# Delta rule: the 16x16 diagonal blocks of I + M inverted by DVE, by way of DRAM, in place of three doubling levels on PE

## The chip, the cores and the metric

The kernel runs on one core of a Trainium2 chip. The metric is the device time of one execution in microseconds (us). The engines are PE (matrix products), DVE (elementwise work on 128 partitions), ACT (activation functions, copies, casts), POOL, and SP, which here only issues transfers; 16 DMA engines move the data between DRAM and the on-chip memory.

## The reference, cut to what matters

Two transformer blocks run one after the other on 256 rows of width 1024. The first is a hybrid layer: attention beside a gated delta rule. The second has a mixer of two kinds of attention and then a mixture of 32 experts. Only the delta rule of the first block is touched. Its core, for each of 8 heads and each chunk of rows, is a triangular system:

```python
def gated_deltanet(q, k, v, g, beta):
    ...
    m = jnp.where(strict, jnp.einsum('bhnid,bhnjd->bhnij', k_beta, kc) * decay, 0.0)
    a_mat = m + jnp.eye(c, dtype=m.dtype)
    rhs = jnp.concatenate([vc * bc[..., None], k_beta * jnp.exp(G)[..., None]], axis=-1)
    sol = lax.linalg.triangular_solve(a_mat, rhs, left_side=True, lower=True, unit_diagonal=True)
    u, w = sol[..., :dv], sol[..., dv:]
    ...
```

The result u, w then feeds a recurrence over the chunks. The inputs q, k, v come from one projection of the normalised input, a causal convolution of width 4, and silu.

## The kernel before

**The first block** takes about the first 400 us. Its big matrix `w_in` is read in pieces of 1 MB (512 rows by 512 columns of float32). A piece is loaded by `load()` (L110, on SP's queue, three buffers), and `piece()` splits it in two parts: ACT casts it to the rounded half `whi` (L309), DVE subtracts to get the rest `wlo` (L310). PE then multiplies with three products for each pair of operands, hi x hi, hi x lo, lo x hi: `proj_T_g` (L204 to L206, 48 products with 256 columns for a piece, output transposed) and `proj_tok_g` (L168 to L170, with 512 columns, output by rows). Near the start stands a small load of the same matrix, 16 columns for beta and the decay: 128 x 8 runs of 64 bytes, 64 KB. The convolution's evacuation on DVE (L533, L535, L540) follows every pair of pieces of the q, k, v of the delta rule.

**The delta rule** is written as a generator, `gdn_half`, for half of the heads (4) at a time. The kernel's chunk is 128 rows, so there are two, t = 0 and 1. For each, the decayed product M is formed transposed, as MT (L604 the product, L605 the decay mask). T, the inverse of I + M, is then built by doubling: blocks of size s on the diagonal are already inverted, and one level joins two neighbours into a block of 2s. The levels are 2, 4, 8, 16, 32, 64; the start is the inverse of the 2x2 blocks, which is I - M with one entry of each block kept (L611, L612 with the table `nm1t`, transposed at L298, copied at L616). One level, for both t and 4 heads, is: 8 + 8 products of MT with the even blocks (L626), a mask on DVE (L628, twice), 8 + 8 products with the transposed T (L641), a subtraction into T on DVE (L642, twice), and, for the next level, 8 transposes of T (L298) with two copies on ACT (L647). The last level, s = 64, ends with L635 and L636 instead. The names in the trace: `Ts` holds T, `TT` its transpose, both among the tiles called `w`.

**The order.** A helper, `together`, runs `gdn_half` and the attention beside the projections: it advances each such generator by one step, then lets the projection go on until 2.5 units of its work are issued. On each engine the order of instructions is fixed when the program is built. Between two groups of a level on PE stand 24 products of a projection. SP issues every load in one order and stands at a load until its buffer is free. The projections of the second half of the heads, the gates and the attention are what runs beside the delta rule; behind them stand the branch products, the mixer, and from about 590 us the experts, which stream 1 MB pieces of weights without a break.

Of the kernel before, what the change touches and what calls it, by code (L numbers as in the profile page):

```python
# [7 lines left out]
F32 = mybir.dt.float32  # L8
# [4 lines left out]
ALU = mybir.AluOpType  # L13
AX = mybir.AxisListType

P = 128
# [1 line left out]
D = 1024  # L18
NEG = -1e30
EPS = 1e-6  # L20
LEVELS = (2, 4, 8, 16, 32, 64)


def _consts():

    import numpy as np

    r = np.arange(P)[:, None]
    c = np.arange(P)[None, :]
    cols = {}  # L30

    cols["ident"] = r == c
    cols["nhalf"] = np.full((P, 16), -0.5)
    cols["iota"] = np.broadcast_to(c[:, :64], (P, 64))
    cols["fold"] = (r % 64) == np.arange(64)[None, :]
    cols["ones"] = np.ones((P, P))
    cols["ustr"] = r < c
    cols["uinc"] = r <= c
    cols["lstr"] = r > c
    cols["cneg"] = np.concatenate([np.zeros((P, P)), np.where(c <= r, 0.0, NEG)], 1)  # L40
    cols["nm1t"] = -((c % 2 == 1) & (r == c - 1)).astype(np.float32)
    lv = []
    for s in LEVELS:
        even = np.array([j for j in range(P) if (j // s) % 2 == 0])[None, :]
        lv.append((r // s == even // s + 1))
    cols["levels"] = np.concatenate(lv, 1)
    half = 16
    inv = np.power(np.float32(500000.0), -np.arange(half, dtype=np.float32) * np.float32(2.0 / 32))
    ang = np.arange(S, dtype=np.float32)[:, None] * inv[None, :].astype(np.float32)
    co, si = np.cos(ang).astype(np.float32), np.sin(ang).astype(np.float32)  # L50
    cols["cosa"] = np.concatenate([co[:P], co[:P], co[P:], co[P:]], 1)
    cols["sina"] = np.concatenate([-si[:P], si[:P], -si[P:], si[P:]], 1)
    inv2 = np.float32(10000.0) ** (-np.arange(0, 32, 2, dtype=np.float32) / np.float32(32))
    cols["inv2"] = np.broadcast_to(inv2[None, :], (P, 16))
    off, at = {}, 0
    for k, v in cols.items():
        off[k] = (at, v.shape[1])
        at += v.shape[1]
    arr = np.ascontiguousarray(np.concatenate([np.asarray(v, np.float32) for v in cols.values()], 1))
    return arr, off  # L60


_CARR, _COFF = _consts()


@with_exitstack
def tile_net(ctx: ExitStack, tc: tile.TileContext, a: dict, dbg=None):
    nc = tc.nc
    V, A, G, T, SY = nc.vector, nc.scalar, nc.gpsimd, nc.tensor, nc.sync
# [13 lines left out]
    def cc(k):  # L83
        o, n = _COFF[k]
        i = max(i for i in range(3) if cuts[i] <= o)
        return ctab[i][:, o - cuts[i]:o - cuts[i] + n]

    ident = cc("ident")
# [207 lines left out]
    def transpose(out, in_):  # L296
        k = in_.shape[0]
        T.transpose(out, in_, ident[:k, :k])  # L298

    def bc(ap, n):  # L300

        return ap[:, :, None].broadcast_to([ap.shape[0], ap.shape[1], n])

    def bm(ap, n):

        return ap[:, None, :].broadcast_to([ap.shape[0], n, ap.shape[1]])
# [92 lines left out]
    with ExitStack() as c1:  # L399
# [4 lines left out]
        w = Pool(wk, **NB)  # L404
# [3 lines left out]
        ps = pm.tile([P, P], F32, name="pm")  # L408
# [21 lines left out]
        ps = pm.tile([P, P], F32, name="pm")  # L430
# [116 lines left out]

        oTb = [None, None]

        def four(f):  # L550
            ps = pm.tile([P, 4, P], F32, name="pm")
            for j in range(4):
                f(j, ps[:, j])
            return ps
# [4 lines left out]
        def gdn_half(hh, cq, ck, cv):  # L559
# [5 lines left out]
            MT, QK, TT, Ts = [], [], [], []  # L565
            for t in range(2):
# [5 lines left out]
                ps = heads4(lambda j: gl[:, j], lambda j: uinc)  # L572
# [4 lines left out]
                for nm, src, sc in (("q", cq, P ** -0.5), ("k", ck, None)):  # L577
                    dst = tk[nm] = w.tile([P, 4, P], F32, name="w2")
                    ps = four(lambda j, o: transpose(o, src[:, j, ts]))
# [4 lines left out]
                    r = rsqrt(ss, 4, 1.0, 4 * EPS, "l_r")  # L584
# [8 lines left out]
                ps = four(lambda j, o: transpose(o, cv[:, j, ts]))  # L593
                V.tensor_tensor(vb[:, t], ps, bc(hbet[:, t, hs], P), ALU.mult)
                yield 0.0
                for src, dst in ((tk["k"], KT[:, :, ts]), (kb, KQ[t][:, :, 0]), (tk["q"], KQ[t][:, :, 1])):
                    ps = four(lambda j, o: transpose(o, src[:, j]))
# [3 lines left out]
                for b in range(2):  # L601
                    ps = pm.tile([P, 2, 2, P], F32, name="pm")
# [3 lines left out]
                                    dm[:, 2 * b:2 * b + 2, None, :].broadcast_to([P, 2, 2, P]), ALU.mult)  # L606
                MT.append(mq[:, :, 0])
                QK.append(mq[:, :, 1])

                tt = w.tile([P, 4, P], F32, name="w2")  # L610
                V.tensor_tensor(tt, MT[t], bm(cc("nm1t"), 4), ALU.mult)  # L611
                V.tensor_tensor(tt, tt, bm(ident, 4), ALU.add)  # L612
                yield 0.0
                ps = four(lambda j, o: transpose(o, tt[:, j]))
                tn = w.tile([P, 4, P], F32, name="w2")
                A.copy(tn, ps)  # L616
                TT.append(tt)
                Ts.append(tn)
                yield 0.0
            for li, s in enumerate(LEVELS):  # L620
                ev = [Ts[t].rearrange("p h (b o s) -> p h b o s", o=2, s=s)[:, :, :, 0] for t in range(2)]
                ys, pss = [], []
                for t in range(2):
                    ps = pm.tile([P, 4, 64], F32, name="pm")
# [6 lines left out]
                if s == 64:  # L631
                    for t in range(2):
                        ps = pm.tile([P, 4, 64], F32, name="pm")
# [4 lines left out]
                for t in range(2):  # L638
                    ps = pm.tile([P, 4, 64], F32, name="pm")
# [4 lines left out]
                for t in range(2):  # L644
                    ps = four(lambda j, o: transpose(o, Ts[t][:, j]))
                    tt = w.tile([P, 4, P], F32, name="w2")
# [6 lines left out]
            ps = heads4(lambda j: TT[0][:, j], lambda j: vb[:, 0, j])  # L653
            A.copy(vn[0], ps)
            yield 0.0
            ps = heads4(lambda j: kdec[:, j], lambda j: vn[0][:, j])
# [1066 lines left out]
```

## Time and profile before

| | us |
|---|---|
| median of 3 runs | 1589.14 (1588.45 to 1589.35) |
| the profiled execution | 1589.79 |
| its span in the trace | 1588.0 |
| PE busy in the span | 1456.5 (92%) |
| DVE busy | 621.5 (39%) |
| ACT busy | 421.8 (27%) |

The span is the time from the first to the last recorded instruction; the execution has 1.79 us around it. PE's share of 92% is an average over stages with different limits, so the windows below count more than the table. DVE and ACT have much idle time in total, spread over the span in short gaps between operations.

### The profile page before, as it was taken

The page shows a single profiled execution, that of the slowest core. Times are in us where ns is not written, and L with a number is a line of the kernel's source. Part 1 is how long each engine was busy: PE and PEld are TensorE (multiplying, and loading weights), DVE is VectorE, ACT ScalarE, POOL GpSimd, SP SyncE. Part 2 cuts the span into 40 slices and gives each one's busy share as a digit, 9 for nine tenths or more (in the row PEclk, how much of TensorE's full clock was granted, in tenths as well). Part 3 has the DMA queues.
Part 4 walks back from the last instruction along what each step waited for, and adds up shares of the span by engine and source line. Part 5 has one row for each costly group of instructions (what it writes and reads, how often), then busy time and mean ns, then how long its engine had stood idle before and what let it go on. Part 6 is the DMA issues. An engine that isn't in the chain of part 4 may idle for free. (4 is left out here: it accounts for less than half of the span.)

```text
span 1588.0 us, 20479 instructions
## 1 busy us (share of the span) xinstructions
PE 1456.5 (92%) x8162; PEld 902.3 (57%) x8162; DVE 621.5 (39%) x1183; ACT 421.8 (27%) x648; POOL 26.0 (2%) x39
## 2 busy tenths in 40 slices
PE   6999999999979989999889989899998889898877
PEld 5889899999779875433424433443443344232325
DVE  6867766456746653302212202221322121220226
ACT  4553554344546631101101101110111010010014
POOL 0000010000000000000000000000000000000000
PEclk9999999999989989999999999999999999999998
DMA  6433233345525179999999999999999999999982
GB/s 211 160 133 124 90 107 107 108 139 193 175 83 186 54 275 388 421 420 421 420 421 419 420 420 421 421 421 420 420 420 421 420 420 420 421 420 421 421 339 93
DMA packets 99247, 484.89 MB, mean 305 GB/s; under 512 B 10470, under 2 KB 14060, under 8 KB 49996
## 3 DMA queue, kind: packets, MB, share of 16 engines
q1 hardware_dynamic: 99004, 483.14, 76.6%
q8 instruction: 66, 1.08, 0.3%
q0 software_dynamic: 144, 0.39, 0.1%
q14 instruction: 33, 0.27, 0.0%
HBM read 482.46 MB, written 1.05 MB: 304 GB/s over the span
## 5 line engine op out<-in xcount | busy, mean ns | idle before, releaser
L1316 PE MATMUL ph<-raw,xs 128*64 128x512 f32 x928 | 233.7, 596 | 6.7 <-DMA raw<-in_w_gu_dram 6.6
L1316 PE MATMUL ph<-whi,xs 128*64 128x512 f32 (+1 forms) x568 | 192.8, 594 | 1.4 <-DMA whi<-in_w_gu_dram 1.3
L1316 PE MATMUL ph<-wlo,xs 128*64 128x512 f32 (+1 forms) x552 | 187.3, 594 | 3.4 <-DMA wlo<-in_w_gu_dram 3.3
L310 DVE TENSOR_TENSOR wlo<-raw,whi 128x2048 fp32r<-128x2048 f32 (+4 forms) x73 | 158.0, 2166 | 79.8 <-ACT whi L309 79.6
L204 PE MATMUL pm<-w,whi 128*128 128x256 f32 x640 | 183.3, 287 | 2.9 <-ACT w L309 2.0
L205 PE MATMUL pm<-w,whi 128*128 128x256 f32 x640 | 180.3, 282 | 2.2 <-DVE w L310 2.2
L206 PE MATMUL pm<-w,wlo 128*128 128x256 f32 x640 | 179.9, 282 | 2.6 <-DVE wlo L310 2.6
L1503 DVE COPY hs<-ph 128x512 f32<-128x512 f32 x34 | 23.5, 692 | 405.0 <-PE ph L1316 405.0
L309 ACT CAST whi<-raw 128x2048 fp32r<-128x2048 f32 (+4 forms) x73 | 132.0, 1808 | 156.2 <-PE pm L205 90.0
L1316 PE MATMUL pm<-raw,act 128*64 128x512 f32 x528 | 150.4, 611 | 23.7 <-DMA raw<-in_w_dn_dram 23.0
L1316 PEld LDWEIGHTS ph<-raw,xs 128*64 128x64 f32 x928 | 74.7, 138 | 141.9 <-issue 127.2
L1503 ACT COPY hs<-ph 128x512 f32<-128x512 f32 x34 | 19.9, 585 | 413.3 <-PE ph L1316 413.3
L1406 DVE SCALAR_TENSOR_TENSOR yl<-pm,gs,yh 128x512 fp32r<-128x512 f32 x34 | 25.4, 749 | 265.1 <-ACT yh L1405 264.4
L204 PEld LDWEIGHTS pm<-w,whi 128*128 128x128 f32 x640 | 122.3, 191 | 3.7 <-ACT w L309 2.4
L206 PEld LDWEIGHTS pm<-w,wlo 128*128 128x128 f32 x640 | 122.6, 192 | 3.1 <-DVE wlo L310 3.0
L205 PEld LDWEIGHTS pm<-w,whi 128*128 128x128 f32 x640 | 122.5, 191 | 2.9 <-DVE w L310 2.8
L1316 PEld LDWEIGHTS ph<-whi,xs 128*64 128x64 f32 (+1 forms) x568 | 62.0, 140 | 83.6 <-issue 76.9
L1316 PE MATMUL pm<-whi,act 128*64 128x512 f32 (+1 forms) x248 | 95.3, 611 | 13.6 <-DMA whi<-in_w_dn_dram 13.6
L1316 PEld LDWEIGHTS ph<-wlo,xs 128*64 128x64 f32 (+1 forms) x552 | 59.3, 140 | 85.0 <-issue 77.4
L1316 PE MATMUL pm<-wlo,act 128*64 128x512 f32 (+1 forms) x248 | 95.0, 597 | 11.4 <-DMA wlo<-in_w_dn_dram 11.4
L1316 PEld LDWEIGHTS pm<-raw,act 128*64 128x64 f32 x528 | 44.9, 139 | 103.7 <-issue 60.6
L1405 ACT ACTIVATE yh<-pm,gs 128x512 fp32r<-128x512 f32 x34 | 23.2, 686 | 282.1 <-PE pm L1316 280.6
(395 smaller groups left out, 1988.7 us busy)
## 6 DMA issues: line engine op xcount, KB each, us to landing
raw<-in_w_gu_dram SPq DMA_DIRECT2D x116, 1024.0 KB, 19.8
whi<-in_w_gu_dram SPq DMA_DIRECT2D x71, 1024.0 KB, 19.8
wlo<-in_w_gu_dram SPq DMA_DIRECT2D x69, 1024.0 KB, 19.9
raw<-in_w_dn_dram SPq DMA_DIRECT2D x66, 1024.0 KB, 19.8
raw<-in_w_in_dram SPq DMA_DIRECT2D x46, 1024.0 KB, 5.1
wlo<-in_w_dn_dram SPq DMA_DIRECT2D x31, 1024.0 KB, 19.8
whi<-in_w_dn_dram SPq DMA_DIRECT2D x31, 1024.0 KB, 19.7
raw<-in_w_branch_a_dram SPq DMA_DIRECT2D x4, 1024.0 KB
```

Of the source, the lines that this page charges most:

```text
L204: T.matmul(o, hi[:, k, ns], xh[:, k0 + k], start=first, stop=False)
L205: T.matmul(o, hi[:, k, ns], xl[:, k0 + k], start=False, stop=False)
L206: T.matmul(o, lo[:, k, ns], xh[:, k0 + k], start=False, stop=last)
L309: A.copy(hi, src)
L310: (by or V).tensor_tensor(lo, src, hi.bitcast(F32), ALU.subtract)
L1316: return tc.keep_in_program_order(T.matmul(*x_, **y_))
L1405: A.activation(yh[:, ns], yp[n_], AF.Copy, scale=b["gs"])
L1406: V.scalar_tensor_tensor(yl[:, ns], yp[n_], b["gs"], yh[:, ns].bitcast(F32), ALU.mult, ALU.subtract)
L1503: (V.tensor_copy if j // 2 else A.copy)(b["hs"][j // 2][:, j % 2 * 512:j % 2 * 512 + 512], hp[j])
```

## The change

The levels are cut to 16, 32 and 64. In place of the three lower ones the 64 blocks of 16x16 on the diagonals (2 chunks x 4 heads x 8 blocks) are inverted by DVE, one block on one partition, by forward elimination: a copy of identities, then for each of 15 columns one multiplication and one subtraction. Since a block's rows lie on 16 partitions, they are moved through DRAM: MT is written out (256 KB for each t), the blocks are read as 64 partitions of 16 rows of 64 bytes, and the inverses are written into a DRAM tile of zeros, from which two full tiles of T are read back. From them TT comes by transposes, as before.

```diff
-LEVELS = (2, 4, 8, 16, 32, 64)
+LEVELS = (16, 32, 64)
+B = 16
...
-    cols["nm1t"] = -((c % 2 == 1) & (r == c - 1)).astype(np.float32)
...
+    cols["eyes"] = np.broadcast_to(np.eye(B).reshape(1, B * B), (P, B * B))
...
+        BS = B * P + B
+        dr = c1.enter_context(tc.tile_pool(name="dr", bufs=1, space=bass.MemoryType.DRAM))
+        whole = dr.tile([8, P // B * BS], F32, name="whole")
+        diag = dr.tile([8, P // B * BS], F32, name="diag")
+        def plain(d, t):
+            return d[t * 4:t * 4 + 4, :P * P].rearrange("h (r c) -> r h c", c=P)
+        def blocks_of(d):
+            v = d.rearrange("g (b r) -> (g b) r", r=BS)[:, :BS - B]
+            return v.rearrange("g (i c) -> g i c", c=P)[:, :, :B]
+        zero = w.tile([P, 4, P], F32, name="w2")
+        V.memset(zero, 0.0)
+        for t in range(2):
+            SY.dma_start(plain(diag, t), zero)
+        def inverse(X, out):
+            V.tensor_copy(out, cc("eyes")[:64].rearrange("p (r c) -> p r c", r=B))
+            tmp = w.tile([P, B, B], F32, name="w1")[:64]
+            for j in range(B - 1):
+                n, m = B - 1 - j, j + 1
+                o = out[:, m:, :m]
+                V.tensor_tensor(tmp[:, :n, :m], bc(X[:, j, m:], m), bm(out[:, j, :m], n), ALU.mult)
+                V.tensor_tensor(o, o, tmp[:, :n, :m], ALU.subtract)
...
                                     dm[:, 2 * b:2 * b + 2, None, :].broadcast_to([P, 2, 2, P]), ALU.mult)
                 MT.append(mq[:, :, 0])
                 QK.append(mq[:, :, 1])
-
+                SY.dma_start(plain(whole, t), MT[t])
+                yield 0.0
+            X = w.tile([P, B, B], F32, name="w1")[:64]
+            SY.dma_start(X, blocks_of(whole))
+            yield 0.0
+            Y = w.tile([P, B, B], F32, name="w1")[:64]
+            inverse(X, Y)
+            yield 0.0
+            SY.dma_start(blocks_of(diag), Y)
+            yield 0.0
+            for t in range(2):
+                tn = w.tile([P, 4, P], F32, name="w2")
+                SY.dma_start(tn, plain(diag, t))
+                Ts.append(tn)
+            yield 0.0
+            for t in range(2):
+                ps = four(lambda j, o: transpose(o, Ts[t][:, j]))
                 tt = w.tile([P, 4, P], F32, name="w2")
-                V.tensor_tensor(tt, MT[t], bm(cc("nm1t"), 4), ALU.mult)
-                V.tensor_tensor(tt, tt, bm(ident, 4), ALU.add)
-                yield 0.0
-                ps = four(lambda j, o: transpose(o, tt[:, j]))
-                tn = w.tile([P, 4, P], F32, name="w2")
-                A.copy(tn, ps)
+                A.copy(tt, ps)
                 TT.append(tt)
-                Ts.append(tn)
-                yield 0.0
+            yield 0.0
             for li, s in enumerate(LEVELS):
                 ev = [Ts[t].rearrange("p h (b o s) -> p h b o s", o=2, s=s)[:, :, :, 0] for t in range(2)]
                 ys, pss = [], []
```

The table of constants that is loaded at the start shrinks by 64 columns. In the lines of after, which are the same code some lines later, PE's products are L205 to L207 (projection) and L669, L684 (the level), the transposes L299, DVE's split L311 and MT's product with its mask L635, L636.

On PE, in the first half, a level's groups and the fills between them. Before, `w_843` and `w_1051` are MT of the two chunks, `w_872` and `w_1103` are T:

```order
L206 MATMUL pm<-w_88,wlo 128x256
L626 MATMUL pm<-w_872,w_843 128x64 x4
L626 MATMUL pm<-w_1103,w_1051 128x64 x4
L204 MATMUL pm<-w_89,whi 128x256
...
L206 MATMUL pm<-w_89,wlo 128x256
L641 MATMUL pm<-w_1134,w_852 128x64 x4
L641 MATMUL pm<-w_1141,w_1060 128x64 x4
```

After, at the place where the first transposes of the blocks' inverses stand (`w_1185` and `w_1187` are the two tiles read back), 12 products L169 to L171 and 196 of L205 to L207 behind the second chunk's L635:

```order
L635 MATMUL pm<-w_678,w_679 128x256 x4
L169 MATMUL pm<-whi,w_89 128x512
...
L205 MATMUL pm<-w_88,whi 128x256
L299 MATMUL pm<-C_66,w_1185 128x128 x4
L206 MATMUL pm<-w_90,whi 128x256
L207 MATMUL pm<-w_88,wlo 128x256
L205 MATMUL pm<-w_88,whi 128x256
L299 MATMUL pm<-C_66,w_1187 128x128 x4
L669 MATMUL pm<-w_1185,w_851 128x64 x4
L669 MATMUL pm<-w_1187,w_1038 128x64 x4
```

The 24 products that stood between two groups of a level have moved together into one long run ahead of the transposes; behind it some groups have 3 between them, others 23 to 26. In the second half 192 projection products stand there, together with transposes and 8 products of the attention.

On DVE, the same place. Before, between MT's mask and the second level (`xpad` belongs to the convolution):

```order
L605 TENSOR_TENSOR w_1051<-pm,w_892 128x512 x2
L310 TENSOR_TENSOR wlo<-raw,whi 128x2048
L611 TENSOR_TENSOR w_1060<-w_1051,C_144 128x512
L612 TENSOR_TENSOR w_1060<-w_1060,C_66 128x512
L628 TENSOR_TENSOR w_1134<-pm,C_144 128x256
L628 TENSOR_TENSOR w_1141<-pm,C_144 128x256
L310 TENSOR_TENSOR wlo<-raw,whi 128x2048
L642 TENSOR_TENSOR w_872<-w_872,pm 128x128x2
```

After, `w_1060` are the blocks and `w_1097` their inverses:

```order
L636 TENSOR_TENSOR w_1038<-pm,w_873 128x512 x2
L573 COPY w_1097<-C_144 64x256
L311 TENSOR_TENSOR wlo<-raw,whi 128x2048
L578 TENSOR_TENSOR w_1099<-w_1060,w_1097 64x15
L579 TENSOR_TENSOR w_1097<-w_1097,w_1099 64x15
...
L578 TENSOR_TENSOR w_1099<-w_1060,w_1097 64x8x8
L311 TENSOR_TENSOR wlo<-raw,whi 128x2048
L579 TENSOR_TENSOR w_1097<-w_1097,w_1099 64x8x8
L534 TENSOR_SCALAR w_1064<-xpad,vT 128x256
...
L579 TENSOR_TENSOR w_1097<-w_1097,w_1099 64x15
L311 TENSOR_TENSOR wlo<-raw,whi 128x2048
```

One split stands ahead of the 30 operations, one in the middle of them, and the next behind the last; from the middle on the convolution's operations alternate with them. In the second half the operations of the attention's softmax stand among them instead, with two splits ahead of the inverse and one in it.

On SP's queue, where before 38 loads of `w_in` stand in a row, after:

```order
L640 DMA whole<-w_851 128x4x128
L111 DMA raw<-in_w_in_dram 128x4x512 x3
L640 DMA whole<-w_1038 128x4x128
L645 DMA w_1060<-whole 64x16x16
L111 DMA raw<-in_w_in_dram 128x4x512 x2
L650 DMA diag<-w_1097 64x16x16
L111 DMA raw<-in_w_in_dram 128x4x512
L654 DMA w_1185<-diag 128x4x128
L654 DMA w_1187<-diag 128x4x128
L111 DMA raw<-in_w_in_dram 128x4x512 x6
```

The new transfers have come in among the loads, and each waits at its place for what it moves: L645 for both writes of `whole`, L650 for the inverse, L654 for L650.

## Rows read from the trace of the kernel before

**Rows 1.** The windows: busy us per engine, PE clock, DMA share, GB/s, of two stretches
```profile
100.00:400.00 300.00, 297.45 (x2404) 286.37 (x2403) 188.14 (x269) 139.51 (x189) 9.06 (x9) 1.00 0.39 127
590.00:1520.00 930.00, 852.80 (x3996) 358.64 (x3995) 209.15 (x504) 102.50 (x165) 1.92 (x3) 0.99 1.01 419
```

**Rows 2.** The waits from 100 to 400 us: engine, line, releaser, total us, times, longest
```profile
PE pm L298 <- DVE w L684: 1.7, 2, 1.5
PE pm L205 <- DVE w L310: 0.3, 1, 0.3
...
DVE wlo L310 <- ACT whi L309: 47.8, 19, 5.2
```

**Rows 3.** PE's timeline through one level: start us, duration, operation
```profile
116.05 1.89 PE L626 MATMUL pm<-w,w 128*128 128x64 f32 x16
117.95 0.28 PE L205 MATMUL pm<-w,whi 128*128 128x256 f32 x1
...
120.66 1.90 PE L641 MATMUL pm<-w,w 128*128 128x64 f32 x16
...
122.56 0.28 PE L205 MATMUL pm<-w,whi 128*128 128x256 f32 x1
...
125.27 1.03 PE L298 MATMUL pm<-C,w 128*128 128x128 f32 x8
...
126.26 0.28 PE L205 MATMUL pm<-w,whi 128*128 128x256 f32 x1
```

**Rows 4.** The groups by line up to 560 us: busy us, mean ns of one
```profile
L626 PE MATMUL pm<-w,w 128*128 128x64 f32 x192 | 22.7, 271 | 0.0
...
L641 PE MATMUL pm<-w,w 128*128 128x64 f32 x160 | 18.9, 271 | 0.0
...
L628 DVE TENSOR_TENSOR w<-pm,C 128x256 f32<-128x256 f32 x24 | 10.1, 423 | 17.2 <-PE pm L626 17.2
```

**Rows 5.** DVE's timeline, near 22, 110 and 130 us
```profile
22.92 0.18 DVE L456 TENSOR_SCALAR angk<-ang 128x32 f32<-128x32 f32 x1
23.13 0.18 DVE L457 TENSOR_SCALAR angk<-angk 128x32 f32<-128x32 f32 x1
...
109.95 0.69 DVE L605 TENSOR_TENSOR w<-pm,w 128x512 f32<-128x512 f32 x1 [0.17 <-PE pm L604]
110.56 2.29 DVE L310 TENSOR_TENSOR wlo<-raw,whi 128x2048 fp32r<-128x2048 f32 x1
...
130.10 0.61 DVE L533 TENSOR_SCALAR w<-xpad,vT 128x256 f32<-128x256 f32 x2
130.63 2.46 DVE L535 SCALAR_TENSOR_TENSOR w<-xpad,vT,w 128x256 f32<-128x256 f32 x6
```

**Rows 6.** Transfers: SP's issue, the windows, the list of DMA issues
```profile
16.38 0.43 SPq L110 DMA_DIRECT2D raw<-in_w_in_dram  x1
...
18.00:19.00 1.00, 0.99 (x4) 1.00 (x5) 1.00 (x2) 0.21 (x1) 0.00 (x0) 0.50 0.73 57
...
raw<-in_w_in_dram SPq DMA_DIRECT2D x46, 1024.0 KB, 5.1
...
out_dram<-hs SPq DMA_DIRECT2D x4, 256.0 KB, 2.2
```

**Rows 7.** The windows around three stretches in which PE stood
```profile
16.10:18.00 1.90, 0.00 (x0) 0.00 (x0) 1.90 (x3) 1.76 (x1) 0.00 (x0) 0.89 0.19 17
19.00:20.50 1.50, 1.50 (x9) 1.50 (x8) 1.50 (x1) 0.00 (x0) 0.00 (x0) 0.50 0.85 276
...
436.00:439.00 3.00, 0.00 (x0) 0.00 (x0) 1.06 (x3) 1.92 (x5) 0.55 (x1) 1.00 0.00 0
441.00:447.00 6.00, 5.38 (x17) 4.87 (x18) 2.98 (x7) 1.44 (x3) 0.55 (x1) 0.50 0.00 0
450.00:452.00 2.00, 0.24 (x3) 0.08 (x1) 2.00 (x2) 0.80 (x3) 0.00 (x0) 1.00 0.00 0
```

## The prediction, made blind

> **What bounds the kernel now.** I read three views in this order: the busy time by stretch, the waits of the engine that is busiest there, and the timeline of that engine around the changed code. By stretch there are two regimes. From 100 to 400 us, where both halves of the delta rule lie, PE is busy 297.45 of 300 us and the DMA engines carry only 0.39 of what they could; from 590 us to the end of the experts the DMA engines are full (1.01) [rows 1]. So the changed code sits in a stretch that PE sets, and whatever PE is spared there moves everything behind it forward, the expert stream included, since its buffers come free that much earlier. The waits say the same: PE waits 1.7 us for the delta rule's output and 0.3 us for a split piece in 300 us, while DVE waits 47.8 us for ACT's casts [rows 2], that is, DVE has slack, but slack handed out in small portions.
>
> **What is removed.** Three of six levels, in two halves. One level on PE is two groups of 16 products and one of 8 transposes, and between the groups stand 24 projection matmuls, which I call fills. From the second fill after one group to the next group are 23 fill steps: 120.66 - 117.95 = 2.71 us, 0.118 each; 24 cost 2.83. From the start of L626's group to the second fill behind it are 1.90 us, less one step 1.79; for L641's group the same 1.79; for the transposes 0.99 - 0.12 = 0.87 [rows 3]. A level is 4.45 us of PE, three are 13.35, and both halves 26.7. The counts confirm that six levels are there: L626 192 = 6 x 2 x 16 products, L641 five times as many as 32 [rows 4]. Since PE waits for nothing there, this is time of the span. On DVE the masks and subtractions of these levels, 0.42 us each [rows 4], and the two old passes over MT (L611, L612) go; DVE isn't the bound there, so I count that at nothing.
>
> **What is added, and whether it is covered.** The new chain of one half is: MT to DRAM, the 16x16 blocks back to 64 partitions, 31 dependent DVE operations, the blocks to DRAM, two tiles back, transposes. It hides behind the fills that the program puts between the last MT matmuls and those transposes. I count from t0, the end of these matmuls.
>
> First half, PE: 12 fills of 512 columns (as two of 256, 0.236 each: 2.8 us) and 196 of 256 columns (23.1 us): PE arrives at the transposes at t0 + 26. The pieces of 48 fills (5.7 us) begin at 2.8, 8.5, 14.1 and 19.8, and each needs its split on DVE first.
>
> First half, DVE and DMA, from rows: two MT operations of 0.69 [rows 5], to 1.4. A 256 KB write to DRAM lands in 2.2 us [rows 6] (the output's), with 0.4 of issue: 4.0. For the reading of 1024 runs of 64 bytes the nearest row is a load with as many runs of 64 bytes, issued at 16.38, with its traffic in 18 to 19 us (share 0.73, 57 GB/s) [rows 6], so about 2.5 us: 6.4 to 6.9. Meanwhile the second piece is split (2.29 a piece [rows 5]), which stands ahead of the inverse on DVE and waits for its cast; I put its end at 7.8. Then 30 small operations. Dependent ones on 128x32 start 0.21 apart (22.92 to 23.13) [rows 5]; the upper bound is an operation on 128x256 at 0.42 [rows 4]. The inverse's views have 14 to 64 elements a partition, so I take 0.21: 6.3 us. In between stand another split (2.2) and 4 + 10 operations of the convolution (0.61 for two, 2.46 for six [rows 5]: 5.3). Sum: 21.6. Only then comes the split of the piece that PE wants at 19.8; in part the small operations fit between the others' dependences, so I take its end at 23.0 and **a PE stall of 3.2 us** (2 to 4). The blocks' write goes out at about 21.5; no row shows 64-byte runs written to DRAM, and I take the load's 2.5 us, the lower bound being the 2.2 of the plain write and the upper open (rival C). Then a 1 MB load, which SP has queued ahead, and the two 256 KB reads: 1 MB takes 5.1 us to land [rows 6], so the reads land about 29 us, just when the stalled PE arrives: **0.5 us** (0 to 2).
>
> Second half: 192 fills and 2.7 us of transposes stand in between: PE arrives at t0 + 25.4. A third split stands ahead of the inverse, which starts at about 10.8, shares DVE with five softmax operations and a split, and ends near 21.4; the write lands at 24, the reads behind their 1 MB load at 27 to 30. **Stall 3.0 us** (1.5 to 4.5).
>
> Three small items. In the remaining levels only 3 fills (0.35 us) instead of 24 now stand at some joints, while a pair of DVE operations takes 0.75: **1.5 us** in both halves (0 to 3). The zeroing of one 128x512 tile on DVE and its two writes stand in the start-up, where PE waits for DVE's first split: **0.5** (0.1 to 0.7, the longer end being any 128x512 operation). And the clock: after PE had been idle from 16.1 to 18.0 us its granted clock was 0.50, the 1.2 GHz level, in 18 to 20.5; after 436 to 439 idle it was 0.50 in 441 to 447; after 450 to 452, with 0.24 busy, it stayed at 2.4 GHz [rows 7]. Two stalls of 3 us lie between these; I let one fall and lose half of 3 us: **1.5** (0 to 6). The additional traffic, some 1.5 MB in 300 us, finds the DMA engines at 0.39 and costs nothing; behind them, SP, which issues all loads in order, stands for some 14 us at the blocks' write for the inverse, with three pieces already loaded (17 us of PE work), so nothing runs dry unless the inverse is late by more than that.
>
> What the Trainium skill says against the 64-byte writes: "DMA: Bandwidth & Descriptors", Specifications, puts the smallest transfer at line rate at 512 bytes and says that below it the engine reads, modifies and writes. No run here shows such a write. If each of them cost the 64-byte load's transfer of about 1 us once more, the estimate by this page would be 2 us on the sum.
>
> **Sum.** 26.7 - (3.2 + 0.5 + 3.0 + 1.5 + 0.5 + 1.5 = 10.2) = 16.5 us. Against the profiled execution, 1589.79 us, that gives 1573.3; it lies 0.65 above the median of the runs shown, so against that 1572.6, and I say **1572.5 us**.
>
> **The rivals.**
> A, all is hidden: splits and reads come in time, as PE's tiny waits of now suggest [rows 2]. Then the whole 26.7 is gained: 1562.4. Against it stands the in-order DVE, which has a split behind the inverse in both halves. Chance 0.13.
> B, DVE becomes the bound: the small operations cost 0.42 instead of 0.21, or the inverse starts later since its blocks come late. 30 x 0.21 = 6.3 us per half more, each of them a stall, since the split behind the inverse is already late: 1572.5 + 12.6 = 1585.1; half of it 1579. Chance 0.14 for 1577 to 1585.
> C, slower: the four transfers with 64-byte runs. Each us that one takes beyond 2.5 is a us on the chain, in both halves, and PE has no more fills to give. From 16.5 / 4 = 4.1 us more each, 6.6 a transfer, the change loses; at 9 us each it is 1572.5 + 26 = 1598.5. For it: 1024 runs with a price not seen in writing. Against it: the load of the same runs had its traffic within about a us. Chance 0.08.
> D, it is no gain since something else sets the end of the stretch, or B and C meet in the middle: 1589. Against it: PE at 297 of 300 us. Chance 0.03.
>
> **How the numbers follow.** My forecast (1566 to 1577) has 0.62. A comparison of this kernel can tell about 0.2%, 3.2 us, from no change. Faster: 0.62 + 0.13 + 0.14 = 0.89; the same: D, 0.03; slower: C, 0.08. The range goes from rival A's end, 1562.5, to the middle of B, 1582, and leaves out the upper part of B, C and D: some 0.17.
>
> **What would show it.** Right: L626's successor runs 96 times instead of 192, PE's waits in 100 to 400 us name a split (L311) late behind the inverse once in each half, some 3 us each, and the transposes wait for the reads by about as much in the second half; the expert stream starts some 16 us sooner and is as long as before. Wrong: the inverse's operations well above 0.21; the writes of blocks landing after 4 us or more; a PE wait of more than 5 us in either half; the clock at its lower level for more than 3 us in the stretch; or a longer start-up than 0.5 us.

## The result, and the profile after

The changed kernel takes **1570.7 us** (median of 4 runs, 1567.5 to 1573.7) against 1588.8 us: a ratio of 0.9892 with a 95% interval of 0.988 to 0.9905. In a later set of runs the same kernel gave 1570.85 us and 0.9903 (0.9888 to 0.9917). The forecast was 1572.5 us in a range of 1562.5 to 1582. The profiled execution of after is the fastest of its four, 1567.49 us, with a span of 1565.7; the account below is of that one, and the profile of after taken later (1570.3 us, near the median) says which parts of it recur.

The waits of PE from 100 to 400 us in after (columns as in [rows 2]):

```profile
PE pm L299 <- DMA w<-diag: 6.2, 2, 5.4
PE pm L207 <- DVE wlo L311: 2.6, 1, 2.6
PE pm L154 <- DVE wlo L311: 0.9, 1, 0.9
```

Where PE waited for 2.5 us in 300 before [rows 2], two new waits stand now: on the tiles read back from DRAM, and on one split. (The third row lies behind the projections and stood near 410 us before.) PE's timeline places them, first half and second half:

```profile
125.25 0.39 PE L207 MATMUL pm<-w,wlo 128*128 128x256 f32 x1 [2.65 <-DVE wlo L311]
131.80 0.66 PE L299 MATMUL pm<-C,w 128*128 128x128 f32 x4 [0.82 <-DMA w<-diag]
...
245.13 1.94 PE L299 MATMUL pm<-C,w 128*128 128x128 f32 x8 [5.38 <-DMA w<-diag]
246.87 3.37 PE L362 MATMUL pm<-w,w 128*128 128x256 f32 x8
```

In the last two rows the transposes and products take about twice as long as elsewhere (8 transposes took 1.03 us in [rows 3]). The windows of after (columns as in [rows 1]) say why: the granted clock fell to 0.5, the 1.2 GHz level, while PE stood, and came back only near 249.9 us, 4.8 us after PE had work again.

```profile
240.00:242.00 2.00, 0.00 (x0) 0.00 (x0) 0.40 (x1) 2.00 (x3) 0.00 (x0) 1.00 0.94 316
242.00:244.00 2.00, 0.00 (x0) 0.00 (x0) 2.00 (x2) 0.56 (x2) 0.00 (x0) 0.76 1.05 343
244.00:246.00 2.00, 0.87 (x4) 0.90 (x5) 1.97 (x3) 0.00 (x0) 0.00 (x0) 0.50 0.79 157
246.00:248.00 2.00, 2.00 (x9) 1.82 (x8) 0.35 (x1) 1.17 (x2) 0.00 (x0) 0.50 1.04 406
248.00:250.00 2.00, 2.00 (x6) 1.56 (x6) 0.69 (x1) 0.00 (x0) 0.00 (x0) 0.54 0.16 62
```

The groups by line up to 560 us in after, which answer to [rows 4]: the level's two groups run 96 and 64 times instead of 192 and 160, and the 60 operations of the inverse take 0.2 us each.

```profile
L669 PE MATMUL pm<-w,w 128*128 128x64 f32 x96 | 11.4, 272 | 0.0
...
L684 PE MATMUL pm<-w,w 128*128 128x64 f32 x64 | 7.6, 271 | 0.0
...
L579 DVE TENSOR_TENSOR w<-w,w 64x15 f32<-64x15 f32 (+7 forms) x30 | 5.9, 197 | 0.6
L578 DVE TENSOR_TENSOR w<-w,w 64x15 f32<-64x15 f32 (+7 forms) x30 | 5.9, 197 | 0.7
```

**A ruler for the stretch.** All projections with output transposed run the same products in all these kernels, and only what stands between them differs. So I count them and compare the start of the 240th, before the delta rule begins, and of the 1248th, well behind it. Between these two stand 1192 other products and transposes in before and 952 in each of the other kernels below, so those differ from one another only in PE's waits, in its clock and in the pace of its products (the mean step from one projection product to the next, where two stand side by side at the full clock). In before's timeline of PE:

```profile
55.17 0.28 PE L206 MATMUL pm<-w,wlo 128*128 128x256 f32 x1
...
350.36 0.28 PE L206 MATMUL pm<-w,wlo 128*128 128x256 f32 x1
```

and the same two products in after:

```profile
53.31 0.28 PE L207 MATMUL pm<-w,wlo 128*128 128x256 f32 x1
...
328.19 0.28 PE L207 MATMUL pm<-w,wlo 128*128 128x256 f32 x1
```

Before takes 295.2 us between them, after 274.9: **the stretch is 20.3 us shorter**. Another 1.9 us lie ahead of it, in the start-up. At the 1680th product the lead is 21.6 us, and the whole span is 22.3 us shorter, so what was gained here was kept to the end: PE's first product of the experts, which the DMA engines set, starts at 576.5 us instead of 598.8, and from there to the end both kernels take 989 us.

Not all of the 20.3 us is the change's. In before's profile the clock was at its lower level from 79.0 to 82.4 us, behind a wait of PE of 1.96 us that ended at 78.8; in after's, behind the same wait, 1.97 us to 77.0, it was not. First before, then after:

```profile
79.00:82.40 3.40, 3.40 (x15) 3.12 (x14) 3.21 (x3) 1.64 (x3) 0.00 (x0) 0.50 0.00 0
79.00:82.40 3.40, 3.40 (x16) 2.74 (x16) 3.40 (x11) 2.28 (x6) 0.00 (x0) 1.00 0.25 46
```

3.4 us of PE's work at half the clock are 1.7 us that before lost and after did not.

### The profile page after: what moved, and what is told of

It reads as the page before. It is cut to its first block, busy times and chain, and to the rows that moved or that the text cites. A ratio compares the mean times of both kernels' runs of the same rounds, so it can differ in the third digit from the quotient of the medians.

```text
span 1565.7 us, 20031 instructions
## 1 busy us (share of the span) xinstructions
PE 1426.0 (91%) x7922; PEld 872.3 (56%) x7922; DVE 617.2 (39%) x1214; ACT 415.6 (27%) x636; POOL 27.9 (2%) x39
## 5 line engine op out<-in xcount | busy, mean ns | idle before, releaser
L311 DVE TENSOR_TENSOR wlo<-raw,whi 128x2048 fp32r<-128x2048 f32 (+4 forms) x73 | 157.9, 2165 | 88.4 <-ACT whi L310 88.3
L205 PE MATMUL pm<-w,whi 128*128 128x256 f32 x640 | 180.8, 283 | 2.9 <-ACT w L310 2.0
L207 PE MATMUL pm<-w,wlo 128*128 128x256 f32 x640 | 178.3, 280 | 5.3 <-DVE wlo L311 5.3
L206 PE MATMUL pm<-w,whi 128*128 128x256 f32 x640 | 179.0, 280 | 2.0 <-DVE w L311 1.9
L1359 PE MATMUL pm<-raw,act 128*64 128x512 f32 x528 | 145.9, 597 | 23.2 <-DMA raw<-in_w_dn_dram 22.6
L207 PEld LDWEIGHTS pm<-w,wlo 128*128 128x128 f32 x640 | 121.0, 190 | 6.0 <-DVE wlo L311 5.9
L205 PEld LDWEIGHTS pm<-w,whi 128*128 128x128 f32 x640 | 121.1, 189 | 3.7 <-ACT w L310 2.4
L1448 ACT ACTIVATE yh<-pm,gs 128x512 fp32r<-128x512 f32 x34 | 23.4, 687 | 279.0 <-PE pm L1359 277.3
## 6 DMA issues: line engine op xcount, KB each, us to landing
raw<-in_w_gu_dram SPq DMA_DIRECT2D x116, 1024.0 KB, 19.8
whi<-in_w_gu_dram SPq DMA_DIRECT2D x71, 1024.0 KB, 19.8
wlo<-in_w_gu_dram SPq DMA_DIRECT2D x69, 1024.0 KB, 19.8
raw<-in_w_dn_dram SPq DMA_DIRECT2D x66, 1024.0 KB, 19.8
wlo<-in_w_dn_dram SPq DMA_DIRECT2D x31, 1024.0 KB, 19.8
whi<-in_w_dn_dram SPq DMA_DIRECT2D x31, 1024.0 KB, 19.8
```

The source lines that it names most:

```text
L205: T.matmul(o, hi[:, k, ns], xh[:, k0 + k], start=first, stop=False)
L206: T.matmul(o, hi[:, k, ns], xl[:, k0 + k], start=False, stop=False)
L207: T.matmul(o, lo[:, k, ns], xh[:, k0 + k], start=False, stop=last)
L311: (by or V).tensor_tensor(lo, src, hi.bitcast(F32), ALU.subtract)
L1359: return tc.keep_in_program_order(T.matmul(*x_, **y_))
L1448: A.activation(yh[:, ns], yp[n_], AF.Copy, scale=b["gs"])
```

## The experiments

One table for all. "Stretch" is the gain between the two products, "start-up" the lead at the 240th, both from one profiled execution against the one profile of before; the ratio is that of the runs.

| run | us, median | ratio (95%) | start-up | stretch |
|---|---|---|---|---|
| after | 1570.7 | 0.9892 (0.988 to 0.9905) | 1.86 | 20.3 |
| after, once more | 1570.85 | 0.9903 (0.9888 to 0.9917) | 0.66 | 19.8 |
| levels left out of before | 1563.98 | 0.9849 (0.9835 to 0.9863) | 2.06 | 26.9 |
| read ahead of the inverse | 1702.2 | 1.0711 (1.0692 to 1.073) | 1.06 | 30.1 |
| zeroing late | 1570.06 | 0.9887 (0.9868 to 0.9906) | 2.80 | 19.1 |
| one column | 1562.25 | 0.9834 (0.9817 to 0.9851) | 0.03 | 27.2 |
| reads on ACT's queue | 1580.34 | 0.9958 (0.9944 to 0.9971) | 1.75 | 9.2 |
| two steps later | 1567.1 | 0.9872 (0.9857 to 0.9887) | 1.32 | 22.3 |
| inverse in steps | 1569.61 | 0.9883 (0.9868 to 0.9898) | 0.98 | 20.5 |
| and one step | 1568.64 | 0.9887 (0.9872 to 0.9903) | 1.50 | 21.6 |
| zeroing late, two steps later | 1565.87 | 0.987 (0.9855 to 0.9886) | 1.67 | 24.2 |

**The three levels left out of the kernel before.** It measures the gain with nothing put in its place.

```diff
-            for li, s in enumerate(LEVELS):
+            for li, s in list(enumerate(LEVELS))[3:]:
```

> The kernel before with the three lower levels simply left out of its loop (part of the inverse is not computed): no trip through DRAM, no inverse on DVE. Theory A (the removed levels are PE's time in a stretch that PE sets, and all the rest of the change only takes some of it back): 1588.8 - 26.7 = 1562, within 2 us. Rival B (part of the removed work was not on the path, the change gained elsewhere, as in the start-up): 1567 or more.

In the stretch 26.9 us, by the same two products:

```profile
53.11 0.28 PE L206 MATMUL pm<-w,wlo 128*128 128x256 f32 x1
...
321.45 0.28 PE L206 MATMUL pm<-w,wlo 128*128 128x256 f32 x1
```

That is the sum of the prediction, 26.7, to 0.2 us, but partly by luck: before's low clock at 79 us, which this run's profile doesn't have either, and a faster pace (0.1153 us a product instead of 0.1157) make some 2.1 us of it, and 1.2 us of additional waits of PE go the other way, so that the levels alone are worth about 26 us, an estimate from these three. The median, 1563.98 us, is just within theory A's 1562 and 2 us. The whole run moved by 23.4 us at the median, less than the profiled execution's 25.8 of span, of which 2.1 are the start-up's: of its lead of 28.9 us at the 1680th product 25.7 are left at the 1848th, in the second block's mixer, and what takes them there no run tells. Rival B falls in the stretch; the change gives back 6.5 us of what can be had there.

**The read ahead of the inverse.** All work of the change, without PE's wait for the trip.

```diff
+            for t in range(2):
+                tn = w.tile([P, 4, P], F32, name="w2")
+                SY.dma_start(tn, plain(diag, t))
+                Ts.append(tn)
             yield 0.0
             Y = w.tile([P, B, B], F32, name="w1")[:64]
             inverse(X, Y)
             yield 0.0
             SY.dma_start(blocks_of(diag), Y)
-            yield 0.0
-            for t in range(2):
-                tn = w.tile([P, 4, P], F32, name="w2")
-                SY.dma_start(tn, plain(diag, t))
-                Ts.append(tn)
```

> The changed kernel, but the two tiles of T are read from the DRAM tile before the inverse instead of behind it, so they hold zeros, not the inverses (the blocks' inverse is computed and written but never used): all the work of the change, without the wait for the trip. Theory A (PE's wait for the read back, 6.2 us in the profile, and the lower clock after it, some 2.5 us): 1570.7 - 8 = 1563, and no wait of PE on the tiles read; the late split stays or moves. Rival C (DVE is too busy in this stretch whatever PE waits for): 1569 or more, with new waits of PE on DVE.

The total of 1702 us says nothing on the wait: the experts' work depends on the rows that are routed to them, and with other rows other blocks are loaded. The page of this run has 26 MB more to read than before had (482.46 MB), 24 more pieces of expert weights among them:

```profile
HBM read 508.78 MB, written 2.75 MB: 301 GB/s over the span
```

The stretch can be compared, and it is 30.1 us shorter than before, 9.8 more than after. PE's waits from 100 to 360 us are two, and neither is on a read or a split:

```profile
PE pm L684 <- DVE w L671: 1.4, 1, 1.4
PE pm L362 <- ACT w L629: 0.2, 1, 0.2
```

DVE has the same operations to do as in after, so theory A holds over C as far as the sum goes. But two things changed at once: since the order on PE is made by reckoning, it now has 96 products ahead of the first transposes, not 196, and the levels' own work lies among the pieces. That leaves the late split open, which the next runs take up. The gain is also 3.2 us above that of the levels left out, with the same products on PE: 1.1 us of it are fewer waits, some 0.6 the pace, 0.1147 us instead of 0.1153, and the rest is open. (The two other runs that leave out work, "levels left out" and "one column", load as many expert pieces as before, 116 of the largest group, so their totals can be compared.)

**One column of the inverse.**

```diff
-            for j in range(B - 1):
+            for j in range(1):
```

> The changed kernel with 1 of the 15 columns of the inverse (2 operations on DVE instead of 30 in each half; the inverse is incomplete). The order on PE puts the transposes 65 products earlier in the first half and 55 in the second, by its own reckoning of the shorter chain. Theory A (the chain's length is what PE waits for, and the splits behind it): the late split of 2.65 us goes, the read back still waits some 3 us in a half: about 1567. Rival C (DVE's total load sets the stretch, 12.4 us of it go): 1559 to 1562.

The stretch is 27.2 us shorter, 6.9 more than in after: the whole deficit against the levels left out. Among PE's waits from 100 to 360 us the late split is gone; the 0.3 us on a split that is left stands at 356.9 us, far behind, and before has it too [rows 2]:

```profile
PE pm L299 <- DMA w<-diag: 2.3, 2, 1.4
PE pm L206 <- DVE w L311: 0.3, 1, 0.3
```

The write, the 64-byte runs and the read back are all still there, and cost 2.3 us in both halves together. So the trip through DRAM is nearly hidden once the DVE part is short, even with the transposes earlier in the order (65 products in the first half); the reads' remaining wait, 0.9 and 1.4 us, is less than half of the 3 a half that I wrote, and theory A's 1567 is missed. The total, 1562.25, is near rival C's 1559 to 1562, but its mechanism would be DVE's load everywhere; what went is one wait and most of another, so the run alone doesn't separate the two for the first half.

**The inverse in steps.** Five parts of three columns, with a step of the projection between two. On DVE a split now stands ahead of the last columns.

```diff
+                if j in (2, 5, 8, 11):
+                    yield 0.0
...
-            inverse(X, Y)
+            yield from inverse(X, Y)
```

> The changed kernel with the inverse handed out in five parts of three columns, with a step of projection work (24 products) between each two. On DVE the split that was late now stands ahead of the last three columns, on PE 248 products stand ahead of the first half's transposes instead of 196, and on SP the reads follow the blocks' write directly. Theory A (2.65 us of late split, 6.2 us of wait for the reads and 2 us of clock are all that the change gives back): all three go, 1570.7 - 10 = 1560.5. Rival C (DVE's load, or SP standing longer at the blocks' write): new waits of PE on splits or loads, 1568 or more.

Theory A's 1560.5 didn't come: 1569.6, and waits by other names (100 to 360 us):

```profile
PE pm L299 <- DVE w L729: 2.7, 2, 1.8
PE pm L207 <- DVE wlo L311: 1.5, 1, 1.5
PE pm L205 <- ACT whi L310: 1.5, 1, 1.5
PE pm L299 <- DMA w<-diag: 1.2, 1, 1.2
```

The reads' wait went as expected, from 6.2 to 1.2. The late split did not: 1.5 + 1.5 us now stand where 2.65 stood, one on ACT's cast and, 2.3 us later, one on the split. DVE's timeline in this run shows the reason; the first row is the second piece's split, the last two the fourth's and fifth's:

```profile
109.19 2.29 DVE L311 TENSOR_TENSOR wlo<-raw,whi 128x2048 fp32r<-128x2048 f32 x1 [4.30 <-ACT whi L310]
...
114.95 2.28 DVE L311 TENSOR_TENSOR wlo<-raw,whi 128x2048 fp32r<-128x2048 f32 x1
...
124.94 2.28 DVE L311 TENSOR_TENSOR wlo<-raw,whi 128x2048 fp32r<-128x2048 f32 x1
...
128.06 2.28 DVE L311 TENSOR_TENSOR wlo<-raw,whi 128x2048 fp32r<-128x2048 f32 x1
```

DVE first stands 4.3 us, with the blocks not yet read and the piece not yet cast, and from 109.2 us on it has no gap until behind the splits. Putting the split ahead of the last columns puts the convolution's operations ahead of it instead. In this place of the first half, then, rival C fits: what counts is not the split's place behind the inverse but how much DVE has to do there beside PE's work. Taking operations away removed the wait (one column), and so did more of PE's work among the pieces (the read ahead of the inverse, with all of DVE's operations); this reordering did not. Since those two runs also moved the order on PE, this is the reading that fits all three, and none of them shows it by itself. The wait of 2.7 us at L729 is at the delta rule's end, behind the levels that now come later; it is the one that before has at L684.

Two more things keep the stretch from gaining. The clock fell here too, from 128.3 to 131.7 us, 3.4 us of PE's work. And waits and low clock together took 2.4 us less than in after, while the stretch is only 0.2 us shorter: the pace was 0.1157 us a product, in after 0.1142, which is 1.5 us on a thousand. Why, no run shows.

**And one step.** The same with one more step ahead of the transposes.

```diff
             yield 0.0
+            yield 0.0
             for t in range(2):
                 ps = four(lambda j, o: transpose(o, Ts[t][:, j]))
```

> As the run with the inverse in five parts, with one more step ahead of the transposes. Theory A: the same 1560.5, the waits being gone already; were some left in the second half, another 1 to 2 us less. Rival F (the levels, pushed later, run into the attention's and the projections' end, where fewer products are left to hide them): 1563 or more, with waits of PE behind 300 us.

1568.6 us, within the spread of the run before it: a miss of theory A for the same reason. Rival F's 1563 or more holds as a number, but not its reason: no wait behind 300 us names the levels.

**The reads on ACT's queue**, to pass the 1 MB load on SP's.

```diff
-                SY.dma_start(tn, plain(diag, t))
+                A.dma_start(tn, plain(diag, t))
```

> The changed kernel with the two tiles read back on ACT's queue instead of SP's, so that the 1 MB load that SP has queued ahead is passed. The order moves with it: 172 products ahead of the first half's transposes instead of 196, as many as before in the second. Theory A (the 5.4 us wait of the second half is the queue: the blocks' write lands late beside one 1 MB load and the reads stand behind another): the second half's wait falls to 2 to 3 us, 1570.7 - 3 = 1567.5; ACT stands some 2 us at the reads. Rival E (the wait is the write's landing, not the queue, or ACT's standing delays its casts): 1570 or more.

A clear loss against after, 1580.3 us. Theory A is refuted where it was to show: the second half's wait hardly moved, 5.07 us for 5.38:

```profile
257.26 1.08 PE L299 MATMUL pm<-C,w 128*128 128x128 f32 x4 [5.07 <-DMA w<-diag]
```

Rival E's "1570 or more" holds, but neither theory has the size. The other queue passed nothing, since the load had gone out first: SP issued it at 250.85 us and ACT the reads at 252.40, when the blocks' write had landed; in the first half at 126.34 and 126.64. There the reads, issued by 127.6 us, released the first transposes at 134.25 and the second group at 137.28, with the DMA engines at a share of 0.88 in the window from 126 to 134 us: 6.7 us from the issue to the first use, where after has 4.1. The larger part of the loss is the clock. Three waits (3.0 on the split, 3.3 and 1.3 on the reads) stood close together, and from 134 to 146 us all of PE's work ran at the lower level:

```profile
126.00:134.00 8.00, 4.62 (x24) 4.42 (x24) 5.15 (x11) 0.59 (x1) 0.00 (x0) 0.78 0.88 269
134.00:146.00 12.00, 10.47 (x48) 10.18 (x49) 2.68 (x6) 2.22 (x4) 0.00 (x0) 0.50 0.11 41
```

With two shorter drops, from 127.0 to 130.4 and from 256.7 to 260.1 us, PE did 18.2 us of work at half the clock in this run, 9.1 lost, against 4.8 and 2.4 in after. These 6.7 us and some 4 us more of waits make nearly all of the 11.1 us that the stretch lost against after.

**The transposes two steps later.** The reads of the second half then stand ahead of the 1 MB load on SP's queue.

```diff
                 Ts.append(tn)
             yield 0.0
+            yield 0.0
+            yield 0.0
```

> The changed kernel with the transposes placed two steps later in the program (two more yields). On SP the reads of the second half now stand ahead of the 1 MB load, and the wait can only shrink; PE's order ahead of the transposes stays at 196 and some 142 to 145 products. Theory A: the second half's wait falls from 5.4 us to about 2, with no drop of the clock: 1570.7 - 5 = 1565.5. Rival E (the load ahead of the reads is not it): 1570.

1567.1 us (1566.6 to 1568.1 in 4 runs), the stretch 2.0 us shorter than in after. SP's timeline and PE's at that place:

```profile
242.49 0.93 SPq L654 DMA_DIRECT2D w<-diag  x2
243.51 16.48 SPq L111 DMA_DIRECT2D raw<-in_w_in_dram  x3
```

```profile
245.53 0.63 PE L299 MATMUL pm<-C,w 128*128 128x128 f32 x4 [1.74 <-DMA w<-diag]
```

From the end of the issue at 243.42 to the use are 2.1 us, in after 4.2 (240.94 to 245.13). The wait of the second half is 1.74 us instead of 5.38, and the clock stays at 1.00 in the window from 200 to 250 us. So theory A holds, but for part of the gain only: of the 3.6 us that the wait lost, 2.0 are that the reads landed sooner and 1.7 that PE reached the transposes later, both counted from t0 of the second half, since 8 products of the attention (1.89 us) now stand ahead of the transposes and not behind them. Some of what I expected is missing: in this profile PE waits 1.5 us on the reads of the first half (0.82 in after), 3.0 on the split (2.65) and 1.3 at the delta rule's end.

**The zeroing late**, from the start-up into the first half.

```diff
-        zero = w.tile([P, 4, P], F32, name="w2")
-        V.memset(zero, 0.0)
-        for t in range(2):
-            SY.dma_start(plain(diag, t), zero)
...
             MT, QK, TT, Ts = [], [], [], []
+            if hh == 0:
+                zero = w.tile([P, 4, P], F32, name="w2")
+                V.memset(zero, 0.0)
+                for t in range(2):
+                    SY.dma_start(plain(diag, t), zero)
```

> The changed kernel with the zeroing of the DRAM tile moved from the start-up into the first half of the delta rule. Theory A (the zeroing costs the start-up 0.5 us): 1570.2. Rival D (the start-up of the changed kernel is 2 us shorter than before only because the zeroing shifted PE's work so that its clock stayed high at 38 to 42 us): 1572, with the clock at 0.5 there again.

1570.06 us, not to be told from after. The column "start-up" of the table shows how far the start varies from one profile to the next, 0.03 to 2.80 us, and the three runs without the zeroing there have 2.06, 2.80 and 1.67, those with it 0.03 to 1.86. The half microsecond is plausible and not shown. Rival D's drop of the clock at 38 to 42 us didn't come, nor did it in the run with the levels left out, which has no zeroing at all.

**Both, and after once more**, on the same chip.

> The changed kernel with both edits that helped or did no harm: the transposes two steps later and the zeroing out of the start-up. Theory A (the two are independent): the two-steps-later run's 1567.1 less 0.5 to 1 of start-up, 1566.3; PE's waits on the reads some 3 us, on the late split 2.65 to 3. Rival D (what the start-up gains is a matter of the clock's chance, not of the zeroing): 1567 to 1568.

> The changed kernel once more, on the same chip as the run beside it. Theory A: again 1567 to 1574, a wider spread than the kernel before has, since in some executions a stall of PE lets its clock fall and in others not; the median of 1570.7 holds within 1 us. The rival: the first median was off, 1567 or 1573.

Together 1565.87 us, 0.987 (0.9855 to 0.9886), beside 1570.85 of after in the same job: the intervals of the two ratios don't overlap. It has the lowest median of the versions that compute everything, but its ratio is not to be told from that of the two steps alone (0.9872), so what the later zeroing adds is not shown. PE's waits in its profile are 1.5 us on the reads and 2.7 on the split. After itself repeated its median to 0.2 us. Its second profile has the late split (2.8 us) and the second half's wait (4.9 us, with the clock low behind it) again, no wait on the reads in the first half, and one more drop of the clock, from 128.2 to 131.6 us, behind the late split.

## Why the prediction was right

The sum was 26.7 - 10.2 = 16.5 us; measured are 18.1 by the medians, 22.3 by the spans of the two profiles and 19.5 by that of after's second profile. The mechanism held: PE sets the stretch, the levels' time is gained there, and a late split and the read back take part of it. Its sizes held less well. Point by point, against the profile of after:

- **The removed levels**: 26.7 forecast, 26.9 measured with nothing in their place, of which about 26 are the levels' own.
- **The first half's DVE chain.** t0 is at 102.7 us. The split ahead of the inverse ends at t0 + 7.8, as written, and the inverse at t0 + 20.3 instead of 21.6. DVE's timeline (a dependent operation every 0.22 to 0.25 us, and the next piece's split right behind the last of them):

```profile
108.27 2.29 DVE L311 TENSOR_TENSOR wlo<-raw,whi 128x2048 fp32r<-128x2048 f32 x1 [4.30 <-ACT whi L310]
110.52 0.18 DVE L578 TENSOR_TENSOR w<-w,w 64x15 f32<-64x15 f32 x1
110.74 0.18 DVE L579 TENSOR_TENSOR w<-w,w 64x15 f32<-64x15 f32 x1
...
113.94 2.28 DVE L311 TENSOR_TENSOR wlo<-raw,whi 128x2048 fp32r<-128x2048 f32 x1
...
122.83 0.16 DVE L579 TENSOR_TENSOR w<-w,w 64x15 f32<-64x15 f32 x1
122.92 2.28 DVE L311 TENSOR_TENSOR wlo<-raw,whi 128x2048 fp32r<-128x2048 f32 x1
```

  The stall is 2.65 us for 3.2 forecast, the read's 0.82 for 0.5. Its cause was put down as the split's place behind the inverse; the run in steps shows that another place alone doesn't help, and the two runs without the wait fit the reading that the amount of DVE's work beside PE's is what counts. A late split in the second half, which the prediction named as a sign of being right, didn't come.
- **The 64-byte transfers** (rival C) are cheap. In the windows of after, the DMA engines are filled to 0.34 and 0.43 for a us each at the blocks' read (0.69 us of it are the 64-byte packets), and to 0.54 for one at the blocks' write:

```profile
108.00:109.00 1.00, 1.00 (x11) 1.00 (x11) 0.73 (x1) 0.23 (x1) 0.00 (x0) 1.00 0.34 43
109.00:110.00 1.00, 1.00 (x12) 1.00 (x11) 1.00 (x1) 0.00 (x0) 0.00 (x0) 1.00 0.43 39
...
124.00:125.00 1.00, 0.00 (x0) 0.00 (x0) 1.00 (x1) 0.00 (x0) 0.00 (x0) 1.00 0.54 66
```

  The write lands within 2.1 us of its issue's end at 123.6 (the read behind it goes out at 125.7); I had taken 2.5. By the Trainium skill's rule that was weighed ("DMA: Bandwidth & Descriptors", Specifications: below 512 bytes the engine reads, modifies and writes) I had estimated about 1 us more for each write. None of it came: the 1024 packets of a write took 0.54 us of the engines in the first half and 0.70 in the second, those of a read 0.69 and 0.70.
- **The second half** was the term that was mis-sized: 5.38 us for 3.0, beyond its own bound of 4.5. The DVE part was right, the inverse ends at t0 + 21.4 as forecast (236.1 with t0 at 214.7), and PE arrives at 25.0, for 25.4. Both transfers were too short in the sum. SP's timeline:

```profile
236.11 0.60 SPq L650 DMA_DIRECT2D diag<-w  x1
238.41 0.38 SPq L111 DMA_DIRECT2D raw<-in_w_in_dram  x1
240.02 0.92 SPq L654 DMA_DIRECT2D w<-diag  x2
```

  The write lands 3.3 us after its issue. A 1 MB load had been issued ahead of it and filled the engines (0.93 to 1.19 of them in each us from 236 to 239); the write's 64-byte packets run only from 238.4 us on, when the load's are through. The reads land 4.2 us after their issue, behind the next load in the same way. From the inverse's end to the write's landing are 3.9 us for some 2.6 in the sum, and from there to the reads' landing 5.1 for some 4.4. The load ahead of the reads was in the sum, the one ahead of the write was not.
- **The clock** fell once in the profile of after, from 243.0 to 249.9 us: 4.8 us of PE's work at half speed, 2.4 lost for 1.5 forecast. The second profile of after has two drops, so this term differs from one execution to the next.
- **The joints with 3 products** cost nothing that PE's waits show, for 1.5 forecast.
- **The start-up** lost nothing measurable, for 0.5.

What the stalls and the clock took is 2.65 + 6.2 + 2.4 = 11.3 us. That it is so near the 10.2 of the sum is luck in part: the second half cost 2.4 us more than forecast and the clock 0.9, the joints and the start-up 2.0 less. Two of the prediction's own signs of being wrong came true, a wait of PE of more than 5 us in one half (5.38) and more than 3 us at the lower clock in the stretch (6.9); the time lay near the forecast all the same.

The stretch gained 20.3 and not 26.9 - 11.3 = 15.6. PE has the same products there as with the levels left out, so the rest must be other waits, the clock and the pace. The run with the levels left out has 3.0 us of waits that after hasn't, 2.5 of them at the delta rule's end (L684, 1.7 in before), and its pace is 0.1153 us a product, in after 0.1142, some 1.1 us on a thousand. That is 4.1 of the 4.7 us. Why the wait at the end is gone, beyond the new order, and why the pace differs is left open (below). Rival A's full gain, rival B's 0.42 us an operation, rival C's slow 64-byte transfers and rival D's other bound didn't come; the inverse ended 1.3 us sooner than forecast in the first half and at the forecast time in the second.

## What to carry to other kernels

Work taken off an engine that is hardly ever idle was gained here nearly in full, and the sum of its steps on the timeline predicted it to about 1 us; the new chain that replaces it cost only where the order leaves too little of that engine's other work ahead of its end, so count both to the same mark. A round trip through DRAM was mostly hidden here, but each of its transfers was priced by what had been issued ahead of it: put small transfers ahead of big loads in the program. The other queue didn't pass a load that was already out. Stalls of a few us can cost more than their sum, as where PE's clock fell with them (9.1 us lost to the clock with the reads on ACT's queue). And one profile of each kernel carries its own luck: clock and pace alone made differences of 1 to 2 us in the stretch.

## What the runs showed of the hardware

- The write of 1024 runs of 64 bytes to DRAM took 0.54 us of the DMA engines on quiet engines and landed within 2.1 us of its issue's end; behind a 1 MB load on the same queue it took 0.70 and landed in 3.3. The difference lies ahead of its packets: they began 0.65 us after the issue in the one case and 1.7 in the other, when the load's were through, and from the last of them to the landing were at most 0.7 and 0.8 us. The Trainium skill ("DMA: Bandwidth & Descriptors", Latency and other measured facts) says that the latency of HBM makes most of a transfer's fixed cost and grows with load. This trace shows no such growth: the longer landing is the wait behind the load.
- A dependent DVE operation on 64 partitions and 15 to 64 elements starts 0.20 to 0.25 us after the one before it; where an independent operation stands in between, that one starts 0.09 to 0.13 us after it.
- The same projection product starts every 0.113 us in some stretches and every 0.118 in others, at a granted clock of 1.00 in both, and not in the same places from kernel to kernel or in two profiles of one kernel (0.1142 us on average in after, 0.1148 in its second profile). No run here shows what decides it.
- Behind a stall of PE of nearly the same length the clock fell in one execution and not in another: behind 2.65 us in after's first half it stayed at 1.00, behind 2.82 us in its second profile it was at 0.50 from 128.2 to 131.6 us.
